# One-column modulation products placed one by one behind large products

## The chip, the cores and the metric

The kernel runs on one core of a Trainium2 chip. The metric is the device time of one execution in microseconds (us); the value compared is the median of several executions. TensorE (PE) multiplies, VectorE (DVE), ScalarE (ACT) and GpSimd (POOL) do the elementwise work, and SyncE (SP) issues most DMAs. PEld is the part of TensorE that loads weights while a product streams.

## The reference

One encoder layer on 512 tokens of width 2048 in fp32. What the change touches is the beginning: the modulation and the modulated LayerNorm, whose result h feeds every input projection.

```python
mod = jax.nn.silu(c) @ w_ada[l] + b_ada[l]
shift, scale, gate = jnp.split(mod[:, None, :], 3, axis=-1)
h = _layernorm(x) * (1.0 + scale) + shift
proj = h @ w_in[l]
# ... gated MLP on one half of proj, windowed attention on the other
y = jnp.concatenate([y_a, y_b], axis=-1) @ w_out[l]
x = _layernorm(DEEPNORM_ALPHA * x + (1.0 + gate) * y, ln_g[l], ln_b[l])
```

## The kernel before

The contraction dimension of 2048 is cut into 16 slices of 128 channels. h is kept transposed, one tile of 128 channels x 512 tokens for each slice, as two fp32r numbers `h_hi` + `h_lo`; each weight tile is split likewise into `whi` + `wlo` (or `xhi`, `xlo`): the DMA fills `raw`, ACT copies it to `whi` (L199), DVE or POOL subtracts (L201). Every product of the projections is then three "large" TensorE products of 512 (L229) or 256 columns (L242).

In the first part of the program, up to some 217 us, h is not there yet. The projections start with slices 0 and 1 and proceed in segments (`segment`), a segment for each pair of slices; while a segment runs, the modulation of the next pair is prepared. For a pair k0, k0+1 this is:

- `ada_vector`: 16 DVE multiply-adds (L384, L386) over `wada` tiles, and a last addition (L392) that leaves partial sums over 128 partitions in `scratch[1]`, a part of `gate1`.
- `ada_end`: four products of the partial sums with a column of ones (L400) add up the partitions. They are plain fp32, 128 weights columns and one streamed column each, and give shift and scale of the two slices as four columns of a PSUM tile `pc`. DVE adds the bias into `modc` (L401).
- `make_h`: ACT applies shift and scale (L416) and copies to `h_hi` (L417), DVE makes `h_lo` (L418).

There are seven such groups of four, for k0 = 2, 4, ... 14. The text calls them groups 1 to 7.

`pc` comes from `bank()`, which hands out the ring `psx`. Up to 217 us this ring has two PSUM banks (`ps_x`, bufs=2). The same ring serves the partial sums of the projections (`sums`): each sum of six or twelve large products fills one bank, and is then added into SBUF by DVE (L497) or copied by ACT (L491, L494), which frees the bank. The vz products (L242 and some of L229) instead go to four `psm` banks that they keep.

The order on each engine is made when the program is built: a scheduler places instructions by their dependencies and its own estimate of times, and picks the bank of a tile that is free first by that estimate. Instructions marked `pin` keep their order in the program. The first part of the program hands control from `segment` to `prepare` by a count of steps (L545 to L552), one `advance(1)` for each `yield`. Engines work through their instructions in order, so an instruction that waits holds up all that stand behind it on its engine.

Of the kernel before, what the change touches and what calls it, by code (L numbers as in the profile page):

```python
# [2 lines left out]

# [9 lines left out]
ALU = mybir.AluOpType  # L13
# [3 lines left out]
P = 128  # L17
# [54 lines left out]
def hybrid_kernel(ctx: ExitStack, tc: tile.TileContext, x, c, w_ada, b_ada_cols, b_gate, w_in,  # L72
                  sgu_g, sgu_b, w_sp, b_sp, rpb, band_mask, w_out, ln_g, ln_b, out):
    nc = tc.nc
    pin = tc.keep_in_program_order
# [10 lines left out]
    def bank(ring="x"):  # L86
        turn[0] += ring == "m"
        pool = rings[ring][turn[0] % 5 == 0 if len(rings[ring]) > 1 else 0]
        return pool.tile([P, T], F32, name="ps" + ring, tag=ring)
# [9 lines left out]
    bada = const.tile([P, 2, NK], F32, name="bada")  # L99
# [4 lines left out]
    one = ones.bitcast(F32)[:, 0:1]  # L104
# [15 lines left out]
    def tok(t):  # L120
        return slice(t * P, (t + 1) * P)
# [82 lines left out]
    def next_ws(n):  # L204

        while at[1] < len(plan) and len(ready) < depth[0] + (at[1] < BEFORE_LAST):
            split_w()
        return [ready.pop(0) for _ in range(n)]

    def next_w():  # L210
        return next_ws(1)[0]

    def mm3(ps, wl, i, kl, chan_major, first, last, part=slice(0, T), of=lambda i: slice(i, T, 4)):

        hi, lo, k0, widths = wl
        kk = k0 + kl
        col, o = i * P if chan_major else part.start, 0
        for w in widths:
            if col < w:
                break  # L220
            col, o = col - w, o + 2 * w
        cs = slice(o + kl * w + col, o + kl * w + (col + P if chan_major else part.stop))
        if chan_major:
            trip = ((hi[:, cs], h_hi[:, kk, :]), (hi[:, cs], h_lo[:, kk, :]), (lo[:, cs], h_hi[:, kk, :]))
        else:
            t_hi, t_lo = h_hi[:, kk, of(i)], h_lo[:, kk, of(i)]
            trip = ((t_hi, hi[:, cs]), (t_hi, lo[:, cs]), (t_lo, hi[:, cs]))
        for j, (a, b) in enumerate(trip):
            nc.tensor.matmul(ps, lhsT=a, rhs=b, start=first and j == 0, stop=last and j == 2)  # L229

    def mm_vz(ps, wl, i, kl, first, last):

        if i >= 2:
            mm3(ps, wl, i, kl, True, first, last)
            return
        hi, lo, k0, (w, _) = wl
        cs = slice(kl * w, (kl + 1) * w)

        for t in range(2):
            a_hi, a_lo = [h[:, k0 + kl, tok(2 * i + t)] for h in (h_hi, h_lo)]  # L240
            for j, (a, b) in enumerate(((a_hi, hi), (a_hi, lo), (a_lo, hi))):
                nc.tensor.matmul(ps[:, t * w:(t + 1) * w], lhsT=a, rhs=b[:, cs], start=first and t == 0 and j == 0,  # L242
                                 stop=last and t == 1 and j == 2)

    def project(kind, evac):

        pss = [bank("m") for _ in range(4)]
        for ch in range(8):
            wl = next_w()
            for i in range(4):  # L250
                for kl in range(2):
                    ends = ch + kl == 0, ch == 7 and kl == 1
                    if kind == "vz":
                        mm_vz(pss[i], wl, i, kl, *ends)
                    else:
                        mm3(pss[i], wl, i, kl, kind == "c", *ends)
                if ch == 7:
                    evac(i, pss[i])
                yield
# [28 lines left out]
    def vz_products(wl, last, evac=None):  # L288

        for i in range(4):  # L290
            for kl in range(2):
                mm_vz(res[i], wl, i, kl, False, last and kl == 1)
            if last:
                evac(i, res[i])
            yield
# [18 lines left out]
    scratch = [gate1[:, i * T:(i + 1) * T] for i in range(4)]  # L314

    with tc.tile_pool(name="ph1", bufs=1) as ph1:
# [25 lines left out]
        modc = ph1.tile([P, 2, NK], F32, name="modc")  # L342
# [51 lines left out]
        def ada_end(k0, nk):  # L394

            pc = acc_ps[0][:, T - 2:] if nk == 1 else bank()[:, :4]
            pc = pc.rearrange("p (s k) -> p s k", s=2)
            for s in range(2):
                for i in range(nk):
                    nc.tensor.matmul(pc[:, s, i:i + 1], lhsT=scratch[1][:, (nk * s + i) * P:(nk * s + i + 1) * P], rhs=one, start=True, stop=True)  # L400
            nc.vector.tensor_tensor(out=modc[:, :, k0:k0 + nk], in0=pc, in1=bada[:, :, k0:k0 + nk], op=ALU.add)  # L401
            yield
            for kk in range(k0, k0 + nk):
                make_h(kk, nk == 1)
                yield

        def make_h(kk, direct=False):

            xn = xt[:, :, kk * P:(kk + 1) * P]
            h_hi_k, h_lo_k = [h[:, kk, :].rearrange("p (n k) -> p n k", n=NT) for h in (h_hi, h_lo)]  # L410
            sc, bi = modc[:, 1, kk:kk + 1], modc[:, 0, kk:kk + 1]
            if direct:
                nc.scalar.activation(out=h_hi_k, in_=xn, func=AF.Identity, scale=sc, bias=bi)  # L413
                pin(nc.vector.tensor_scalar(out=xn, in0=xn, scalar1=sc, scalar2=bi, op0=ALU.mult, op1=ALU.add))
            else:
                nc.scalar.activation(out=xn, in_=xn, func=AF.Identity, scale=sc, bias=bi)  # L416
                nc.scalar.copy(out=h_hi_k, in_=xn)  # L417
            nc.vector.tensor_tensor(out=h_lo_k, in0=xn, in1=h_hi_k.bitcast(F32), op=ALU.subtract)  # L418

        def prepare():  # L420
            yield from ada_both(0)
            make_h(0, True)
            yield
            yield from ada_vector(1, 1)
            yield from ada_end(1, 1)
            before = iter(())
            for k0 in EVEN[1:]:
                yield from ada_vector(k0, 2, before)
                yield
                before = ada_end(k0, 2)  # L430
            yield from before
# [67 lines left out]
        def sums(q, wls, i, seg):  # L499

            ps = bank()
            for n, wl in enumerate(wls):
                for kl in range(2):
                    mm3(ps, wl, i, kl, accs[q][1], n + kl == 0, n == len(wls) - 1 and kl == 1)
                if n < len(wls) - 1:
                    yield
            sum_evac(q, i, ps, seg)
            yield

        def first_segment():  # L510

            wz, wv = next_ws(2)
            for i in range(4):
                mm_vz(res[i], wz, i, 0, True, False)
            two = [bank() for _ in range(2)]
            for i in range(2):
                mm3(two[i], wv, i, 0, False, True, False)
            advance(6)
            for i in range(4):
                mm_vz(res[i], wz, i, 1, False, False)  # L520
            yield
            for i in range(2):
                mm3(two[i], wv, i, 1, False, False, True)
                sum_evac(V, i, two[i], 0)
                yield
            for i in range(2, 4):
                yield from sums(V, [wv], i, 0)
            for q in SEGMENTS[0][1][2:]:
                wls = next_ws(1)
                for i in range(4):  # L530
                    yield from sums(q, wls, i, 0)
# [339 lines left out]
    with tc.tile_pool(name="ph3", bufs=1) as ph3:  # L871
# [46 lines left out]
        for cg in range(4):  # L918
            last = cg == 3
# [102 lines left out]
```

## Time and profile before

| what | value |
|---|---|
| median of 3 runs (909.05 to 910.12) | 909.17 us |
| the profiled execution: time | 911.18 us |
| the profiled execution: span from first to last instruction | 909.3 us |
| PE busy | 872.9 us, 96% of the span |
| DVE / ACT / POOL busy | 596.1 / 321.3 / 313.7 us |
| granted TensorE clock, mean | 0.987 of full |

The clock is at full (2.4 GHz) from 50 us on, up to the last stretch. From the page one reads which engine is busy throughout, from the chain of waits which engine's work the end follows from, and from the timeline of a few microseconds what each product costs and what it waits for. A product's record is longer than the step to the next one, because records overlap: steps are read as the difference of two starts.

### The profile page before, as it was taken

Reading aid. Unit: us, or ns where it says so; the run is one execution under the profiler, and the core shown is the slowest. Engines: PE = TensorE matmul, PEld = TensorE weight load, DVE = VectorE, ACT = ScalarE, POOL = GpSimd, SP = SyncE. Lnnn points to the kernel's source line nnn. Section 1 sums busy time; section 2 is a strip of 40 time slices with the busy share of each in tenths; the row PEclk is TensorE's granted clock in tenths of the full one; section 3 lists DMA queues with packets and bytes.
Section 4 is the critical chain, followed back from the end, with each engine's and each line's share of the span. In section 5 each row is a group of like instructions: output and inputs, shape, how many; then the busy total and the mean of one; then the engine's idle time right before and its main releaser. Section 6 shows DMA issues by size and latency. Waiting matters only on the chain.

```text
span 909.3 us, 11756 instructions
## 1 busy us (share of the span) xinstructions
PE 872.9 (96%) x4444; PEld 758.2 (83%) x4444; DVE 596.1 (66%) x864; ACT 321.3 (35%) x397; POOL 313.7 (35%) x223
## 2 busy tenths in 40 slices
PE   4799999999999999999999999999999999999993
PEld 3688888887988988898889988998888888888883
DVE  7867899634586546767768677867866625252667
ACT  3363333233641434515262515433262521122200
POOL 5436566236431526044344525252420000000035
PEclk9799999999999999999999999999999999999997
DMA  9999889744332233444454354444342282323213
GB/s 296 334 356 315 280 275 289 220 115 141 99 97 85 79 99 101 137 135 155 128 182 153 113 182 149 144 120 128 112 126 98 87 353 97 108 97 116 70 61 125
DMA packets 107499, 144.56 MB, mean 159 GB/s; under 512 B 7217, under 2 KB 79025, under 8 KB 106673
## 3 DMA queue, kind: packets, MB, share of 16 engines
q1 hardware_dynamic: 103120, 134.25, 46.4%
q10 hardware_dynamic: 4322, 9.55, 3.1%
q8 instruction: 35, 0.57, 0.3%
q14 instruction: 22, 0.18, 0.1%
HBM read 139.58 MB, written 4.19 MB: 158 GB/s over the span
## 4 chain that ended last, share of the span: by engine, by line
PE 64%; POOL 2%; issue 1%; DVE 1%; ACT 1%; DMA 0%; POOLq 0%; SPq 0%; DVEq 0%; ACTq 0%
PE psm L229 52%; PE psm L242 7%; POOL xr L901 1%; PE psx L712 1%; PE psx L664 1%; PE psx L591 1%; PE psx L663 1%; PE psx L710 1%; POOL xr L902 1%; PE psx L711 1%; POOL rs L126 0%; DMA raw<-in_w_in_dram 0%; ACT xr L900 0%; DVE wlo L201 0%; POOLq L1017 0%
## 5 line engine op out<-in xcount | busy, mean ns | idle before, releaser
L199 ACT CAST whi<-raw 128x1024 fp32r<-128x1024 f32 x133 | 139.3, 1050 | 349.6 <-PE psm L229 223.0
L201 DVE TENSOR_TENSOR wlo<-raw,whi 128x1024 fp32r<-128x1024 f32 x94 | 130.2, 1388 | 162.2 <-ACT whi L199 154.3
L229 PE MATMUL psm<-h_hi,whi 128*128 128x512 f32 x444 | 175.5, 396 | 0.4 <-DVE klo L617 0.4
L229 PE MATMUL psm<-h_lo,whi 128*128 128x512 f32 x444 | 173.9, 392 | 0.0
L229 PE MATMUL psm<-h_hi,wlo 128*128 128x512 f32 x444 | 173.8, 391 | 0.0
L201 POOL TENSOR_TENSOR wlo<-raw,whi 128x1024 fp32r<-128x1024 f32 x39 | 93.9, 2412 | 100.4 <-ACT whi L199 76.3
L229 PE MATMUL psm<-whi,h_hi 128*128 128x512 f32 (+1 forms) x296 | 114.7, 388 | 0.0
L229 PE MATMUL psm<-wlo,h_hi 128*128 128x512 f32 (+1 forms) x296 | 114.0, 385 | 0.0
L229 PE MATMUL psm<-whi,h_lo 128*128 128x512 f32 (+1 forms) x296 | 114.0, 385 | 0.0
L229 PEld LDWEIGHTS psm<-h_hi,wlo 128*128 128x128 f32 x444 | 83.8, 189 | 18.0
L229 PEld LDWEIGHTS psm<-h_hi,whi 128*128 128x128 f32 x444 | 83.9, 189 | 16.2 <-issue 0.8
L229 PEld LDWEIGHTS psm<-h_lo,whi 128*128 128x128 f32 x444 | 84.1, 189 | 15.3 <-issue 0.2
L242 PE MATMUL psm<-whi,h_hi 128*128 128x256 f32 x248 | 71.7, 290 | 2.8 <-ACT h_hi L413 2.3
L126 POOL TENSOR_TENSOR rs<-vareps,mhalf 128x1 f32<-128x1 f32 x4 | 4.1, 1026 | 203.5 <-DVE vareps L125 203.5
L386 DVE SCALAR_TENSOR_TENSOR ada<-wada,c_sb,ada 128x512 f32<-128x512 f32 (+1 forms) x104 | 68.9, 713 | 6.8 <-DMA wada<-in_w_ada_dram 6.8
L242 PE MATMUL psm<-whi,h_lo 128*128 128x256 f32 x248 | 70.9, 288 | 1.0 <-DVE h_lo L418 1.0
L242 PE MATMUL psm<-wlo,h_hi 128*128 128x256 f32 x248 | 71.1, 287 | 0.2 <-POOL wlo L201 0.2
L229 PEld LDWEIGHTS psm<-wlo,h_hi 128*128 128x128 f32 x296 | 63.5, 215 | 8.5
L229 PEld LDWEIGHTS psm<-whi,h_lo 128*128 128x128 f32 x296 | 63.4, 214 | 8.5
L229 PEld LDWEIGHTS psm<-whi,h_hi 128*128 128x128 f32 x296 | 63.4, 214 | 8.4
L229 PE MATMUL psx<-h_hi,whi 128*128 128x512 f32 x160 | 63.6, 397 | 1.2 <-DVE y_b L497 0.9
L229 PE MATMUL psx<-h_lo,whi 128*128 128x512 f32 x160 | 62.4, 390 | 0.0
(206 smaller groups left out, 1612.2 us busy)
## 6 DMA issues: line engine op xcount, KB each, us to landing
wada<-in_w_ada_dram SPq DMA_DIRECT2D x128, 256.0 KB, 5.9
raw<-in_w_in_dram SPq DMA_DIRECT2D x128, 256.0 KB, 3.1
raw<-in_w_in_dram SPq DMA_DIRECT2D x48, 512.0 KB, 4.1
rawg<-in_w_ada_dram SPq DMA_DIRECT2D x32, 512.0 KB, 4.3
raw<-in_w_out_dram SPq DMA_DIRECT2D x32, 512.0 KB, 3.6
xt<-in_x_dram SPq DMA_DIRECT2D x8, 512.0 KB, 7.7
xr<-in_x_dram ACTq DMA_DIRECT2D x4, 1024.0 KB, 8.9
tt<-in_rpb_dram ACTq DMA_DIRECT2D x16, 128.0 KB, 2.1
```

Source lines behind the costliest of these rows:

```text
L199: nc.scalar.copy(out=hi, in_=raw)
L201: eng.tensor_tensor(out=low, in0=raw, in1=hi.bitcast(F32), op=ALU.subtract)
L229: nc.tensor.matmul(ps, lhsT=a, rhs=b, start=first and j == 0, stop=last and j == 2)
L242: nc.tensor.matmul(ps[:, t * w:(t + 1) * w], lhsT=a, rhs=b[:, cs], start=first and t == 0 and j == 0, stop=last and t == 1 and j == 2)
L386: nc.vector.scalar_tensor_tensor(out=even if j == NK - 2 else acc, in0=wt[:, j - j0], scalar=cj, in1=acc, op0=ALU.mult, op1=ALU.add)
L591: nc.tensor.matmul(ps[:, tok(n)], lhsT=v[n][:, tok(g)], rhs=wsT[:, g, :], start=True, stop=True)
L663: nc.tensor.matmul(po, lhsT=k2[:, h, keys], rhs=q2[:, h, q], start=True, stop=False)
L664: nc.tensor.matmul(po, lhsT=klo[:, h, keys], rhs=q2[:, h, q], start=False, stop=True)
L710: nc.tensor.matmul(ps[:, q], lhsT=v_hi[:, t, h, :], rhs=hi[:, sl], start=t == 0, stop=False, skip_group_check=True)
L711: nc.tensor.matmul(ps[0:64, q], lhsT=v_lo[:, t, h, :], rhs=hi[:, sl], start=False, stop=False, skip_group_check=True)
L712: nc.tensor.matmul(ps[:, q], lhsT=v_hi[:, t, h, :], rhs=lo[:, sl], start=False, stop=t == 3, skip_group_check=True)
L901: nc.gpsimd.tensor_tensor(out=xr[:, t, cs], in0=xr[:, t, cs], in1=gl[:, cs], op=ALU.mult)
```

## The change

Of the four products and the addition of each group, `ada_end` no longer issues five instructions in a row. It puts them into a list `beside`. Every large product (in `mm3` and `mm_vz`) now goes through `next_beside`: if the list holds something, the large product is pinned and the first entry is issued behind it. So one product stands behind each of the next four large products, and the addition is issued behind the fifth. What is still listed when `prepare` is resumed is issued at once. The pair that is handled as single slices (nk == 1, before the groups) keeps its order, now pinned.

```diff
+    beside = []
+
+    def next_beside(large):
+        if beside:
+            pin(large)
+            beside.pop(0)()
...
-            nc.tensor.matmul(ps, lhsT=a, rhs=b, start=first and j == 0, stop=last and j == 2)
+            next_beside(nc.tensor.matmul(ps, lhsT=a, rhs=b, start=first and j == 0, stop=last and j == 2))
...
-            for s in range(2):
-                for i in range(nk):
-                    nc.tensor.matmul(pc[:, s, i:i + 1], lhsT=scratch[1][:, (nk * s + i) * P:(nk * s + i + 1) * P], rhs=one, start=True, stop=True)
-            nc.vector.tensor_tensor(out=modc[:, :, k0:k0 + nk], in0=pc, in1=bada[:, :, k0:k0 + nk], op=ALU.add)
-            yield
+
+            def product(s, i):
+                pin(nc.tensor.matmul(pc[:, s, i:i + 1], lhsT=scratch[1][:, (nk * s + i) * P:(nk * s + i + 1) * P], rhs=one, start=True, stop=True))
+
+            def columns():
+                nc.vector.tensor_tensor(out=modc[:, :, k0:k0 + nk], in0=pc, in1=bada[:, :, k0:k0 + nk], op=ALU.add)
+            todo = [partial(product, s, i) for s in range(2) for i in range(nk)] + [columns]
+            if nk == 1:
+                for f in todo:
+                    f()
+            else:
+                beside.extend(todo)
+            yield
+            while beside:
+                beside.pop(0)()
```

What the scheduler makes of it is shown at two places. Lines of the changed kernel differ: its L238 is L229 of before, L409 is L400, L200 is L199, L435 is L416, L436 is L417, L510 is L491. A name's last number tells one tile from another, and each `psx` number is one use of a bank.

TensorE at group 3, before: psx_1040 is the sum that ends, psx_1048 holds the four products, psx_1054 is the next sum.

```order
L229 MATMUL psx_1040<-h_hi_90,wlo_877 128x512
L400 MATMUL psx_1048<-ones_75,gate1_92 128x1 [waits DVE_49]
L400 MATMUL psx_1048<-ones_75,gate1_92 128x1 x3
L229 MATMUL psx_1054<-h_hi_90,whi_876 128x512 [waits DVE_49]
L229 MATMUL psx_1054<-h_lo_91,whi_876 128x512
```

The same place in the changed kernel, where psx_1049 is the next sum:

```order
L238 MATMUL psx_1040<-h_hi_90,wlo_877 128x512
L238 MATMUL psx_1049<-h_hi_90,whi_876 128x512 [waits DVE_49]
L409 MATMUL psx_1048<-ones_75,gate1_92 128x1 [waits DVE_49]
L238 MATMUL psx_1049<-h_lo_91,whi_876 128x512
L409 MATMUL psx_1048<-ones_75,gate1_92 128x1
L238 MATMUL psx_1049<-h_hi_90,wlo_877 128x512
```

The next sum now begins ahead of the first product, and two uses of the ring are open side by side while the sum before is still to be emptied. In the built programs psx_1048 had the bank other than that of psx_1040 before, and has the bank of psx_1040 now.

ScalarE behind group 1, before (y_b is the destination of the sums, xt and h_hi belong to slices 2 and 3, xhi to a later weight tile):

```order
L491 COPY s<-psx 128x512 x2
L416 ACTIVATE xt<-xt,modc 128x4x128 x2
L491 COPY y_b_108<-psx 128x512
L417 CAST h_hi<-xt 128x512 x2
L491 COPY y_b_108<-psx 128x512
L199 CAST xhi<-raw 128x1024
```

The same place in the changed kernel:

```order
L510 COPY s<-psx 128x512 x2
L510 COPY y_b_108<-psx 128x512
L435 ACTIVATE xt<-xt,modc 128x4x128 x2
L200 CAST xhi<-raw 128x1024
L436 CAST h_hi<-xt 128x512
L510 COPY y_b_108<-psx 128x512
L436 CAST h_hi<-xt 128x512
```

Shift and scale now come behind one more copy, and the copy to h_hi behind the cast of xhi. On TensorE the first product that reads h of slice 2 (L242, the vz products) stands behind 18 large products counted from the group, where it stood behind 24.

## Rows read from the trace of the kernel before

**Rows 1.** The page: busy time of an engine, and the chain that ended last.

```profile
PE 872.9 (96%) x4444; PEld 758.2 (83%) x4444; DVE 596.1 (66%) x864; ACT 321.3 (35%) x397; POOL 313.7 (35%) x223
PE 64%; POOL 2%; issue 1%; DVE 1%; ACT 1%; DMA 0%; POOLq 0%; SPq 0%; DVEq 0%; ACTq 0%
```

**Rows 2.** The line of the products: durations in ns, first and last start.

```profile
L400 PEld LDWEIGHTS psx<-ones,gate x56: 186/192/192, 61.0 to 201.6; 128*128 128x128 f32 x56
```

**Rows 3.** Timeline at group 6: start, duration (us), engine, line, operation.

```profile
182.12 0.39 PE L229 MATMUL psx<-h_hi,wlo 128*128 128x512 f32 x1
182.12 1.08 PEld L400 LDWEIGHTS psx<-ones,gate 128*128 128x128 f32 x8
182.34 0.95 PE L400 MATMUL psx<-ones,gate 128*128 128x1 f32 x8
183.12 0.19 PEld L229 LDWEIGHTS psx<-h_hi,whi 128*128 128x128 f32 x1
183.24 0.19 PEld L229 LDWEIGHTS psx<-h_lo,whi 128*128 128x128 f32 x1
...
184.16 0.39 PE L229 MATMUL psx<-h_lo,whi 128*128 128x512 f32 x1
```

**Rows 4.** Timeline at group 3.

```profile
109.87 0.39 PE L229 MATMUL psx<-h_hi,wlo 128*128 128x512 f32 x1
110.29 0.69 DVE L497 TENSOR_TENSOR y_a<-psx,y_a 128x512 f32<-128x512 f32 x1
111.04 0.50 PE L229 MATMUL psx<-h_hi,whi 128*128 128x512 f32 x1
...
112.08 0.39 PE L229 MATMUL psx<-h_lo,whi 128*128 128x512 f32 x1
```

**Rows 5.** Timeline at group 4.

```profile
133.62 0.69 DVE L497 TENSOR_TENSOR s<-psx,s 128x512 f32<-128x512 f32 x1 [0.59 <-PE psx L229]
134.37 0.31 PEld L229 LDWEIGHTS psx<-whi,h_hi 128*128 128x128 f32 x1
...
135.54 0.40 PE L229 MATMUL psx<-wlo,h_hi 128*128 128x512 f32 x1
```

**Rows 6.** Timelines at groups 1, 2 and 7: the emptying, then the fifth large product.

```profile
61.41 0.59 ACT L491 COPY s<-psx 128x512 f32<-128x512 f32 x1 [0.70 <-PE psx L229]
63.45 0.40 PE L229 MATMUL psx<-h_lo,whi 128*128 128x512 f32 x1
...
86.26 0.59 ACT L494 COPY gate<-psx 128x512 f32<-128x512 f32 x1 [0.49 <-PE psx L229]
88.12 0.39 PE L229 MATMUL psx<-h_lo,whi 128*128 128x512 f32 x1
...
201.23 0.69 DVE L497 TENSOR_TENSOR s<-psx,s 128x512 f32<-128x512 f32 x1 [2.03 <-PE psx L229]
203.01 0.39 PE L229 MATMUL psx<-h_lo,whi 128*128 128x512 f32 x1
```

**Rows 7.** Timeline of PE at 215 us, where the ring is closed.

```profile
215.52 0.39 PE L229 MATMUL psx<-h_hi,wlo 128*128 128x512 f32 x1
216.78 0.47 PE L229 MATMUL psx<-h_hi,whi 128*128 128x512 f32 x1 [0.88 <-DVE y_b L497]
```

**Rows 8.** Timelines of ACT and PE behind group 1.

```profile
62.39 1.52 ACT L416 ACTIVATE xt<-xt,modc 128x512 f32<-128x512 f32 x2 [0.40 <-DVE modc L401]
64.59 1.14 ACT L417 CAST h_hi<-xt 128x512 fp32r<-128x512 f32 x2
66.11 1.06 ACT L199 CAST xhi<-raw 128x1024 fp32r<-128x1024 f32 x1
67.99 0.28 PE L242 MATMUL psm<-whi,h_hi 128*128 128x256 f32 x1
```

**Rows 9.** Timeline at 173 us: DVE waits for a DMA, PE for DVE.

```profile
173.03 1.42 DVE L386 SCALAR_TENSOR_TENSOR ada<-wada,c_sb,ada 128x512 f32<-128x512 f32 x2 [2.76 <-DMA wada<-in_w_ada_dram]
...
175.09 0.63 PE L229 MATMUL psx<-whi,h_hi 128*128 128x512 f32 x1 [1.65 <-DVE s L497]
```

More of the change, by code (lines that the diff above doesn't have):

```diff
@@ L1 @@
 from contextlib import ExitStack
+from functools import partial
 from itertools import chain
@@ L241, in mm_vz @@
             for j, (a, b) in enumerate(((a_hi, hi), (a_hi, lo), (a_lo, hi))):
-                nc.tensor.matmul(ps[:, t * w:(t + 1) * w], lhsT=a, rhs=b[:, cs], start=first and t == 0 and j == 0,
-                                 stop=last and t == 1 and j == 2)
+                next_beside(nc.tensor.matmul(ps[:, t * w:(t + 1) * w], lhsT=a, rhs=b[:, cs], start=first and t == 0 and j == 0,
+                                             stop=last and t == 1 and j == 2))
     def project(kind, evac):
```

## The prediction

> **What bounds the kernel now.** I read the page first: PE is busy for 96% of the span, and its own work is 64% of the chain that ended last, with no other engine above 2% [rows 1]. So the end moves when PE's stream gets longer or shorter, and I price the change there alone. Next came the line of the products: 56 loads for 28 products, two loads to each [rows 2]. Then I went group by group through the timelines of PE, and asked of each what PE does between the large product that ends one sum and the fifth large product behind it; the changed order has by then issued the same instructions. DVE and ACT came last, since they empty the ring's banks and make h.
>
> **What a product costs.** Group 6 is undisturbed [rows 3]. The next sum's first large product begins when the load for the second starts, at 183.24, and the fifth is at 184.16: a step from one large product to the next is 0.92 / 4 = 0.23 us. In the group each load is 0.19 us long, but loads follow each other faster: from 182.34, where the large product's successor begins, to 183.12 are seven loads, (183.12 − 182.34) / 7 = 0.111 us, and 183.24 − 183.12 is the same. The products' one streamed column vanishes beside that. The first load of the group starts with the last large product at 182.12 and hides under it; the other seven, and the load of the next large product, are exposed. So a group costs 8 × 0.11 = 0.89 us.
>
> **The same products one by one.** Behind a large product, the first load of a single product hides. Its second load, and the load of the large product behind it, have only a one-column product to hide under, and are exposed: 2 × 0.11 = 0.22 us, and four times that is 0.89 us again. The mere taking apart brings nothing. In group 6 I get 184.13 for the fifth large product where it stood at 184.16 [rows 3]; in group 5 likewise −0.02. (A step from large to large with a product between is 0.23 + 0.22 = 0.45 us.) What decides is where the products now find their bank.
>
> **The ring of two banks.** Before, the four products took the bank that had been empty for some time, and while they ran, the sum that had just ended was emptied: group 3 has the last large product at 109.87, the emptying from 110.29 to 110.98, and the next sum's first large product at 111.04, 0.06 us behind it [rows 4]. The products are the cover of that emptying. In the changed order the next sum starts first, in the bank that is free, and the products need the bank of the sum that has just ended. So PE issues one large product and then waits for the emptying, with everything behind the first product in line. The wait ends at the same moment as before; call it W, the end of the emptying plus 0.06. But now the four products are still to come. From W: three exposed loads, 0.33 us, until the second large product starts, then three steps of 0.45, so the fifth large product is at W + 1.67. By group:
>
> - Group 1: ACT ends at 61.41 + 0.59 = 62.00, W = 62.06, fifth large 63.73 against 63.45 [rows 6], +0.28. (Before, PE waited here for the addition of the bias too, so less is lost.)
> - Group 2: 86.26 + 0.59, W = 86.91, 88.58 against 88.12 [rows 6], +0.46.
> - Group 3: W = 111.04, 112.71 against 112.08 [rows 4], +0.63.
> - Group 4: 133.62 + 0.69, W = 134.37. Here h is the weights operand with a stride of four tokens and its load is 0.31 long, not 0.19 [rows 5]. From W to the fifth large product are 1.17 us here and 1.04 in group 3 [rows 4], so an exposed one of these costs 0.13 more. One of them is in each step: the second large product is at W + 0.45, three steps of 0.57 follow, in all 136.53 against 135.54 [rows 5], +0.99.
> - Groups 5 and 6: the large products go to psm banks, or the sum keeps its bank: −0.02 and −0.03.
> - Group 7: 201.23 + 0.69, W = 201.97, 203.64 against 203.01 [rows 6], +0.63.
>
> The sum is +2.9 us. The trace of before shows one wait of just this kind, where the ring is closed at 215 us: PE stands 0.88 us for the emptying by DVE [rows 7]. Five such waits would be 4.4 us, an upper bound for this term; the lower one is nothing, if the emptying begins so early that a large product covers it (it takes 0.59 to 0.69, a large product 0.23).
>
> **h comes later behind group 1.** The addition stands behind the fifth large product now, at about 63.9 to 64.06; before, shift and scale began at 62.39, after 0.40 of waiting for it [rows 8]. ACT then does in order: one copy of a sum (0.59 by [rows 6], until 64.94, since PE ends that sum at about 64.3), shift and scale (1.52), the cast of xhi (1.06), and the first copy to h_hi (1.14 / 2 = 0.57), which makes 68.09. Before, that copy was ready at 64.59 + 0.57 = 65.2 and first read at 67.99 [rows 8], 2.8 us of slack. PE now comes to it after 18 large products from the group instead of 24: 63.73 + 14 × 0.23 = 66.95. It waits 68.09 − 66.95 = 1.14 us, about +1.15. Bounds: nothing, if ACT takes the copies earlier by 1.1 us; 2.1, if the cast of xhi itself is late by another microsecond. I take the sum of the rows. In the other groups h is ready before PE reads it, as I follow it there.
>
> **DVE at 173 us.** An emptying stands there behind multiply-adds that wait 2.76 us for a DMA, and PE waits 1.65 for it [rows 9]. In the changed order one more multiply-add stands ahead of that emptying, but one wada DMA is issued earlier. I take 0, with bounds of −1.65 (the wait goes) and +1.2 (one multiply-add of 0.71 and its DMA's delay).
>
> **The sum.** 2.9 + 1.15 = 4.1 us. The profiled execution was 911.18, so its counterpart would be 915.3; it lay 2.0 above the median of 909.17 (its span leaves 1.9 outside). On the median: 909.17 + 4.1 = **913.3 us**. The bounds of the first two terms give 910.4 to 915.8.
>
> Of what a load may hide under, the trace shows that each starts when the matmul before it starts, one ahead [rows 3]. The Trainium skill, "TensorE: Matmul & The Clock Gate", section "Step-by-step: what each phase is for", says that PE's queue pulls a weight load ahead of running matmuls into a background buffer, so that the next weights load while this product runs. If that reached two loads ahead, a large product would cover both loads of a product; eight loads in a row in group 6, at even distances, speak against it.
>
> **Rivals.**
>
> 1. *A large product covers two loads.* Place: all 28 products; price: one load of 0.111 less for each, −3.1 us. The sum is then +1.0, 910.2 us: not slower by anything that can be told. What can be told is about 0.2%, 1.8 us. It decides once 21 of the 28 products save a load (4.1 − 21 × 0.111 = 1.8). For it: a large product lasts 0.23 and two loads take 0.22. Against it: the even spacing in [rows 3]. A chance of 0.15.
> 2. *h is in time at group 1.* ACT's casts are placed such that shift, scale and the first h_hi come through by 66.9. Then only the ring's part is left: 909.17 + 3.0 = 912.1. For it: 2.8 us of slack before. Against it: the cast of xhi, which is now ahead in ACT's order. A chance of 0.18.
> 3. *DVE's queue at 173 us gets later*, by the extra multiply-add: +1.2, 914.5. For it: PE already waits there [rows 9], so all of it is paid. Against: the DMA that ends the wait is issued earlier. A chance of 0.12.
> 4. *The wait at 173 us goes*, since the DMA that ends it starts earlier, and the change does not do what it says at the ring: there the emptying has run under the large product that now stands first. Then −1.65 + 1.15 or less, 908.7 and below. Against it: an emptying of 0.6 to 0.7 doesn't fit under 0.23. A chance of 0.05.
>
> The forecast keeps 0.50, with a range of its own of 912.3 to 914.1. Cases 2 and 3 are slower too: 0.80 in all. Within 0.2%: 0.15. Faster: 0.05, for rival 4. The range of 8 in 10 takes in the upper half of what rival 1 may give, and leaves out the rest of it, rival 4, and the far ends of the bounds: 910.6 to 914.8.
>
> **What the changed profile must show.** At groups 1 to 4 and 7, the first product waits for DVE or ACT (0.3 to 0.7 us idle of PE, the releaser the emptying), at 5 and 6 not. Steps of 0.45 us between large products with a product between, 0.57 at group 4; steps near 0.34 would mean rival 1. A wait of PE of about 1 us for ACT's h_hi near 67 us; without it, rival 2. Near 173 us a wait between 0 and 2.9. If products stand with no wait at the ring, the bank is not the one I read in the built programs, and the sum loses 2.9.

## The result and the profile after

The changed kernel takes 917.27 us (median of 6 executions, 915.14 to 920.40) where the kernel before took 909.28 beside it: a ratio of 1.009 with a 95% interval of 1.0072 to 1.0107. Three further measurements gave ratios of 1.0078, 1.0089 and 1.009. I had forecast 913.3 and a range up to 914.8: the direction was right, the size half of what came, and the range too narrow.

The page of the changed kernel hardly shows it (parts 1 and 4). PE is busy for the same share of the span as before [rows 1], and has the same share of the chain that ended last:

```profile
PE 876.4 (96%) x4444; PEld 758.9 (83%) x4444; DVE 600.7 (66%) x864; ACT 321.2 (35%) x397; POOL 313.7 (34%) x223
PE 64%; POOL 2%; issue 1%; DVE 1%; ACT 1%; DMA 0%; POOLq 0%; SPq 0%; DVEq 0%; ACTq 0%
```

The list of PE's waits up to 225 us (who waited for whom: us in total, times, longest) shows what is new. Before, this list held the 1.65 us wait of [rows 9], the 0.88 us wait of [rows 7], and 0.3 us for the addition. The products themselves (L409) now wait, in five places, each time for the emptying of a sum, and PE waits for h_hi, h_lo and a second time for a sum y_b:

```profile
PE psx L238 <- DVE s L516: 1.7, 1, 1.7
PE psx L238 <- DVE y_b L516: 1.6, 2, 0.9
PE psx L409 <- DVE s L516: 1.2, 2, 0.6
PE psm L251 <- ACT h_hi L436: 0.8, 1, 0.8
PE psx L409 <- DVE y_a L516: 0.6, 1, 0.6
PE psx L409 <- ACT s L510: 0.5, 1, 0.5
PE psx L409 <- ACT gate L513: 0.4, 1, 0.4
PE psm L251 <- DVE h_lo L437: 0.2, 1, 0.2
```

Group 3 on PE's timeline (start, duration, engine, line, operation), to be held against [rows 4]: one large product, the wait, and then single products with large ones between them.

```profile
111.44 0.39 PE L238 MATMUL psx<-h_hi,whi 128*128 128x512 f32 x1
112.38 0.38 PE L409 MATMUL psx<-ones,gate 128*128 128x1 f32 x2 [0.56 <-DVE y_a L516]
112.63 0.49 PE L238 MATMUL psx<-h_lo,whi 128*128 128x512 f32 x1
...
113.09 0.47 PE L238 MATMUL psx<-h_hi,wlo 128*128 128x512 f32 x1
...
114.00 0.47 PE L238 MATMUL psx<-h_lo,whi 128*128 128x512 f32 x1
```

From the end of the wait, at 112.38, to the fifth large product at 114.00 are 1.62 us; I had reckoned 1.67 from W. The step between large products with a product between them is 113.09 − 112.63 = 0.46, forecast 0.45.

**The ledger.** PE issues the large products in nearly the same order in both kernels. So one can number them, leave the one-column products out, and take the difference of start times of the same number in the two traces: where that difference rises, time is lost. Below, each column is one traced execution of the changed kernel against the first trace of before (a step is the rise between two such numbers, in us). Products of 256 columns start 0.12 us apart and those of 512 columns 0.23, and the two orders mix them differently behind groups 1 and 2; there a row ends where both kernels have issued the same products. Group 4 is counted to its fifth large product, the other groups to the sixth, which comes a step of 0.32 instead of 0.23 behind the fifth.

| place | forecast | trace 1 | trace 2 | trace 3 | trace 4 |
|---|---|---|---|---|---|
| start of the program, to 61 us | 0 | −1.62 | −1.67 | −0.48 | +3.58 |
| group 1 | +0.28 | 0.30 | 0.30 | 0.31 | 0.30 |
| h behind group 1, to 73 us | +1.15 | 1.53 | 1.52 | 1.53 | 1.52 |
| 73 to 86 us | 0 | 0.27 | 0.28 | 0.27 | 0.25 |
| group 2 | +0.46 | 0.47 | 0.48 | 0.48 | 0.46 |
| 89 to 99 us | 0 | 0.39 | 0.38 | 0.39 | 0.40 |
| group 3 | +0.63 | 0.67 | 0.66 | 0.67 | 0.66 |
| group 4 | +0.99 | 0.82 | 0.81 | 0.81 | 0.81 |
| behind group 4, the next ten large products, the sixth first | 0 | **1.74** | 0.22 | 0.22 | 0.22 |
| the wait at 173 us | 0 | 0.03 | −1.22 | 0.14 | 0.74 |
| group 7 | +0.63 | 0.67 | 0.67 | 0.67 | 0.67 |
| behind group 7 | 0 | 0.69 | −0.07 | 0.18 | 0.32 |
| groups 5, 6 and all else | −0.05 | 0.07 | 0.10 | 0.12 | 0.19 |
| sum behind 61 us | +4.1 | 7.65 | 4.13 | 5.79 | 6.54 |
| time of this execution | | 917.20 | 913.64 | 916.46 | 921.26 |

### The profile page after: what moved, and what is told of

It reads as the page before. It is cut to its first block, busy times and chain, and to the rows that moved or that the text cites. A ratio compares the mean times of both kernels' runs of the same rounds, so it can differ in the third digit from the quotient of the medians.

```text
span 915.4 us, 11754 instructions
## 1 busy us (share of the span) xinstructions
PE 876.4 (96%) x4444; PEld 758.9 (83%) x4444; DVE 600.7 (66%) x864; ACT 321.2 (35%) x397; POOL 313.7 (34%) x223
## 4 chain that ended last, share of the span: by engine, by line
PE 64%; POOL 2%; issue 1%; DVE 1%; ACT 1%; DMA 0%; POOLq 0%; SPq 0%; DVEq 0%; ACTq 0%
PE psm L238 52%; PE psm L251 7%; POOL xr L920 1%; PE psx L731 1%; PE psx L683 1%; PE psx L610 1%; PE psx L682 1%; PE psx L729 1%; POOL xr L921 1%; PE psx L730 1%; POOL rs L127 0%; DMA raw<-in_w_in_dram 0%; ACT xr L919 0%; DVE wlo L202 0%; POOLq L1036 0%
## 5 line engine op out<-in xcount | busy, mean ns | idle before, releaser
L200 ACT CAST whi<-raw 128x1024 fp32r<-128x1024 f32 x133 | 139.2, 1050 | 347.0 <-PE psm L238 229.9
L238 PE MATMUL psm<-h_hi,whi 128*128 128x512 f32 x444 | 175.6, 396 | 0.4 <-DVE klo L636 0.4
L238 PE MATMUL psm<-h_hi,wlo 128*128 128x512 f32 x444 | 173.8, 392 | 0.0
L238 PE MATMUL psm<-h_lo,whi 128*128 128x512 f32 x444 | 173.7, 391 | 0.0
L238 PE MATMUL psm<-whi,h_hi 128*128 128x512 f32 (+1 forms) x296 | 114.7, 388 | 0.0
L238 PE MATMUL psm<-wlo,h_hi 128*128 128x512 f32 (+1 forms) x296 | 114.0, 385 | 0.0
L238 PE MATMUL psm<-whi,h_lo 128*128 128x512 f32 (+1 forms) x296 | 114.0, 385 | 0.0
L238 PEld LDWEIGHTS psm<-h_hi,wlo 128*128 128x128 f32 x444 | 83.6, 188 | 17.8
L238 PEld LDWEIGHTS psm<-h_hi,whi 128*128 128x128 f32 x444 | 84.0, 190 | 16.0 <-issue 0.8
L238 PEld LDWEIGHTS psm<-h_lo,whi 128*128 128x128 f32 x444 | 83.9, 189 | 15.4 <-issue 0.2
L251 PE MATMUL psm<-whi,h_hi 128*128 128x256 f32 x248 | 71.8, 291 | 3.6 <-ACT h_hi L432 2.3
L251 PE MATMUL psm<-whi,h_lo 128*128 128x256 f32 x248 | 70.6, 288 | 1.1 <-DVE h_lo L437 1.1
L251 PE MATMUL psm<-wlo,h_hi 128*128 128x256 f32 x248 | 70.9, 287 | 0.0
L238 PEld LDWEIGHTS psm<-wlo,h_hi 128*128 128x128 f32 x296 | 63.5, 215 | 8.5
L238 PEld LDWEIGHTS psm<-whi,h_lo 128*128 128x128 f32 x296 | 63.4, 214 | 8.5
L238 PEld LDWEIGHTS psm<-whi,h_hi 128*128 128x128 f32 x296 | 63.4, 214 | 8.4
L238 PE MATMUL psx<-h_hi,whi 128*128 128x512 f32 x160 | 63.2, 395 | 1.6 <-DVE y_b L516 1.6
L238 PE MATMUL psx<-h_hi,wlo 128*128 128x512 f32 x160 | 62.9, 393 | 0.4 <-POOL wlo L202 0.4
```

The lines of the kernel that those rows point to most:

```text
L200: nc.scalar.copy(out=hi, in_=raw)
L238: next_beside(nc.tensor.matmul(ps, lhsT=a, rhs=b, start=first and j == 0, stop=last and j == 2))
L251: next_beside(nc.tensor.matmul(ps[:, t * w:(t + 1) * w], lhsT=a, rhs=b[:, cs], start=first and t == 0 and j == 0, stop=last and t == 1 and ...
```

## Experiments

All are short edits of the changed kernel. The times beside them are medians; before took 909.3 to 910.1 in the same sittings. Lines of code that aren't shown are those of the diff ahead.

**The changed kernel three more times** (no edit).

> The changed kernel once more, for a second trace and a tighter time. Theory A (the fall of the granted clock to half at 139.0 to 142.4 us, behind group 4, belongs to the changed order there): the clock falls at the same place again, and the time is about 8 us above before. Rival B (the fall is an event of one execution): no fall at group 4, or one somewhere else, and a time that scatters by some 1.7 us (3.4 us at half speed) from run to run.

> The changed kernel a third time, to see one of its longer executions (918 to 920 us) in a trace. Theory A: the longer ones have a fall of the clock at group 1 too (62 to 70 us), where PE stands still for the ring and then for h, and lose 1.7 us or twice that by it. Rival B: they have the clock of the others there, and lose the time in waits for DMAs or DVE further on (at 173 us up to 1.7, at 228 us 0.7).

> The changed kernel, a fourth trace. Theory A: without a fall of the clock 4 to 6 us of PE's steps behind 60 us more than before, with one at group 4 1.7 us on top; the waits at the groups, behind group 1 and at 95 us as in its other traces. Rival B: the waits themselves differ between executions by a microsecond or more, so that the sum read from one trace says little.

They took 917.13, 918.14 and 918.68 us (ratios of 1.0078, 1.0089 and 1.009) and gave traces 2 to 4 of the table. The losses at the groups, behind group 1 and at 95 us agree to 0.03 us in all four: they belong to the order. Four things differ between executions: the start of the program, the wait at 173 us, what follows group 7 (in trace 1 PE waits there for POOL's `wlo`), and what follows group 4. Trace 1 against trace 2 is the reading for that last one. PE's timeline of trace 1, at group 4 and behind it:

```profile
136.51 0.38 PE L409 MATMUL psx<-ones,gate 128*128 128x1 f32 x2 [0.55 <-DVE s L516]
136.75 0.60 PE L238 MATMUL psx<-wlo,h_hi 128*128 128x512 f32 x1
...
137.33 0.60 PE L238 MATMUL psx<-whi,h_lo 128*128 128x512 f32 x1
...
139.31 0.63 PE L238 MATMUL psx<-whi,h_hi 128*128 128x512 f32 x1
139.74 0.63 PE L238 MATMUL psx<-wlo,h_hi 128*128 128x512 f32 x1
...
142.58 0.40 PE L238 MATMUL psx<-whi,h_lo 128*128 128x512 f32 x1
142.81 0.40 PE L238 MATMUL psx<-whi,h_hi 128*128 128x512 f32 x1
```

Within the group the step is 137.33 − 136.75 = 0.58, as forecast (0.57). Behind it, it is 0.43 at 139.3 and 0.23 at 142.6, and nothing is waited for. The busy times by stretch (start:end, length, then PE, PEld, DVE, ACT, POOL, the granted clock, DMA share, GB/s) say why: the clock fell to half, 1.2 GHz, between 139 and 142, behind a stretch in which PE worked 3.45 of 4 us and had the slow steps of group 4.

```profile
135.00:139.00 4.00, 3.45 (x18) 3.01 (x17) 1.69 (x4) 0.32 (x2) 2.36 (x1) 1.00 0.28 89
139.00:142.00 3.00, 3.00 (x9) 2.35 (x9) 1.77 (x3) 2.41 (x4) 0.00 (x0) 0.50 0.95 298
```

That is 1.74 − 0.22 = 1.5 us of the 7.65. In traces 2 to 4 the same waits are there and the clock holds, so theory A (the fall belongs to the order and comes each time) is wrong as I put it: the fall came in one of these four. What the third trace was to catch, a longer execution with a fall at group 1, wasn't caught. The longest, trace 4, lost its time elsewhere: at the start of the program, 3.58 us. There the clock of 40 to 50 us was lower than in trace 3 (the columns as above; trace 4 first, then trace 3):

```profile
40.00:50.00 10.00, 7.76 (x26) 6.39 (x27) 8.90 (x14) 1.75 (x2) 2.36 (x1) 0.51 1.10 349
```

```profile
40.00:50.00 10.00, 10.00 (x37) 9.00 (x38) 8.93 (x15) 3.75 (x5) 3.93 (x2) 0.73 1.10 350
```

**All groups but the fourth, and the fourth alone.** One condition in `ada_end` each: the group is issued at once.

```diff
-            if nk == 1:
+            if nk == 1 or k0 == 8:      (all but group 4)
+            if k0 != 8:                 (group 4 alone)
```

> The changed order everywhere but at group 4, whose four products stand together again. Theory A (clock fall is caused at group 4): the fall goes, and with it 1.74 us, and the wait and the exposed strided loads of group 4, 0.82: 2.6 us below the changed kernel, some 5.4 us above before. Rival B (the fall is not tied to group 4): 0.8 us below the changed kernel, and the clock falls in another place.

> The kernel before with the changed order at group 4 alone. Theory A: +0.85 us for the wait on the emptied bank and the order of the loads, and +1.74 us for a fall of the clock behind it: +2.6 us. Rival B (no fall without the other groups): +0.85 us, and a clock that stays at full from 50 us on.

> The kernel with the changed order at group 4 alone, a second trace. Theory A: the clock falls at group 4 again in this kernel (its seven times lay within 1.5 us, at 2.2 us above before, which only holds with a fall in nearly all), +2.2 us. Rival B: no fall in this trace, and the 2.2 us are found in steps or waits elsewhere.

Without group 4: 915.28 (ratio 1.0059, 1.0047 to 1.0071), no fall of the clock behind 50 us up to the last stretch, 1.9 us below the changed kernel's 917.13, between theory A's 2.6 and rival B's 0.8. Group 4 alone: 912.08 (1.0026, 1.0016 to 1.0037), and the clock fell at 135.3 us; in the second trace, of a measurement at 911.41 (1.0012, 1.0000 to 1.0024), it held. The two traces in the stretch of the fall, first and second:

```profile
135.00:139.00 4.00, 4.00 (x13) 3.28 (x12) 1.62 (x4) 2.55 (x4) 0.00 (x0) 0.57 0.85 260
```

```profile
135.00:139.00 4.00, 4.00 (x20) 3.91 (x19) 1.97 (x4) 2.38 (x4) 0.42 (x1) 1.00 0.56 168
```

In the ledger the group itself costs 0.82 and 0.81 in both. The fall needs no other group, and comes in some executions. With the changed order at group 4 it was in two of seven traces (the four above, these two, and that of all groups but the first, below). In the ten traces with group 4 as before, or with its products together, there was none, three traces of before among them. Two of seven against none of ten does not settle whether the order at group 4 makes a fall likelier. And a fall does not need that order: both kernels with a slow DVE, below, had one at 133 us, ahead of group 4, and one of them has all its groups together.

**The first group alone, and all but the first.** The same condition, with k0 == 2.

> The kernel before with the changed order at group 1 alone. Theory A (the ring costs 0.30 there, and h_hi and h_lo of slices 2 and 3 come too late behind ScalarE's cast of xhi, 1.6): +1.9 us, with a wait of PE of some 0.8 us for ScalarE's copy to h_hi. Rival B (h is late only because of something further on or of this execution): +0.3 us, and no such wait.

> The kernel with group 1 alone in the changed order once more, for the same question: two of its eight executions were 3 us above the others. Theory A: in such an execution the clock falls between 62 and 75 us. Rival B: the clock stays at full, and a wait elsewhere is longer. If the profile falls on one of the common executions: no fall, and +2.6 us against before in PE's own steps, as in its first trace.

> The changed order everywhere but at group 1, whose four products stand together again. Theory A (group 1 alone costs 2.6 us: the ring 0.3, h_hi and h_lo late 1.6, a later sum of y_b at 95 us 0.6; and the runs some 3 us above the others, seen in the changed kernel and in the one with group 1 alone, come from group 1 too): some 4.7 us below the changed kernel's median, +3 to +4 us against before, no run that stands 3 us above the others. Rival B (the scattered runs come from elsewhere): about 2.6 us below the changed kernel, with runs 3 us apart still there.

Group 1 alone: 912.68 (1.0035, 1.0022 to 1.0048) and 912.42 (1.0023, 1.0011 to 1.0034). The ledger has 0.31 and 0.30 for the ring, 1.52 for h, 0.28 up to 86 us, and then 0.30 between 89 and 99. All but group 1: 913.21 (1.0034, 1.0022 to 1.0047), with 0.14 us between 89 and 99. In the ledger the two parts add up to the whole to 0.05 us there, and most of the loss at 95 us comes with group 1, though it lies 30 us behind it; but PE waits 0.51 us for that emptying without group 1 too. The medians don't add up: the parts are 2.3 to 3.0 and 3.1 us above before, the whole 7.4 to 8.8. None of these three traces shows a clock below full at group 1, so the executions 3 us above the others (before has such ones too, 913.1 to 913.5 in three of 23) stay without an explanation from this place; trace 4 suggests the start of the program, and does not prove it.

**Together, but at the new place.** All four products behind the first large product of the next sum; empty entries keep the next large products in their order.

```diff
-                beside.extend(todo)
+                beside.extend([lambda: [f() for f in todo]] + 4 * [lambda: None])
```

> All four products of each group together, right behind the first large product of the next sum (that large product and the four behind it are kept in this order). Theory A (the place is what costs, by the wait for the bank; being apart costs nothing): PE waits at groups 1 to 4 and 7 as in the changed kernel, the groups cost 2.9 to 3.0 us together, the addition comes three large products earlier and h behind group 1 costs less than 1.6: between +3 and +5 us against before, with falls of the clock behind group 4 in some executions. Rival B (being apart costs by itself): the same waits, but 1 us or more cheaper in the groups than the changed kernel, and no fall of the clock.

> The kernel before with group 4 alone placed so: its four products together, right behind the first large product of the next sum. Theory A (the clock falls because of the stretch without streamed columns, and that is as long whether the products are apart or together): +0.85 us in the group and +1.7 us for a fall of the clock in most executions, about what group 4 alone cost in the changed order, 2.4 us. Rival B (a stretch of slow steps with single products is what takes the clock down): +0.85 us and no fall.

All groups: 913.90 (1.0047, 1.0029 to 1.0066). Group 4 alone (k0 != 8 at once): 910.91 (1.0013, 1.0002 to 1.0023). PE at group 3, which is at the same place as in the changed kernel to 0.03 us:

```profile
111.47 0.39 PE L238 MATMUL psx<-h_hi,whi 128*128 128x512 f32 x1
112.42 1.05 PE L409 MATMUL psx<-ones,gate 128*128 128x1 f32 x8 [0.56 <-DVE y_a L516]
113.33 0.48 PE L238 MATMUL psx<-h_lo,whi 128*128 128x512 f32 x1
...
114.11 0.40 PE L238 MATMUL psx<-h_lo,whi 128*128 128x512 f32 x1
```

The wait is the same, 0.56, and the fifth large product is at 114.11 here and at 114.00 there. In the ledger the groups cost 0.29, 0.46, 0.65, 0.66 and 0.69, where the products apart cost 0.30, 0.47, 0.67, 0.82 + 0.22 and 0.67. So standing apart is free, as worked out, except at group 4 with its strided loads: 0.38 us more. What the changed kernel loses beyond this one lies behind the groups: h behind group 1 costs 0.87 here and 1.53 there, the 0.27 up to 86 us isn't there, and between 89 and 99 us this kernel gains 0.18 where that one loses 0.39. PE does not wait for h_hi here; it waits 0.59 us for h_lo. The clock held in both traces; with one execution each that tells little on whether a fall is likelier with products apart.

**A bank of their own.** The odd multiply-adds accumulate in SBUF, and the bank that this sets free takes the four columns. Once with the products apart, once together at the old place.

```diff
-            accs = [t[:, :2 * w].rearrange("p (s w) -> p s w", s=2) for t in acc_ps]
+            ...
+            if nk == 2:
+                accs[1], even = even, accs[0]
-            pc = acc_ps[0][:, T - 2:] if nk == 1 else bank()[:, :4]
+            pc = acc_ps[0][:, T - 2:] if nk == 1 else acc_ps[1][:, :4]
```

> The changed order, but the four columns get a PSUM bank of their own (the odd multiply-adds accumulate in SBUF, which sets that bank free). Theory A (the ring of two banks is what the products wait for): no wait at any group, eight exposed loads in each, the five groups cost 0.1 to 0.3 us less than before each instead of 2.95 more together, and no fall of the clock behind group 4, since PE does not stand still there. The late h behind group 1 stays (up to 1.6): between -1 and +1.5 us against before. Rival B (single products cost by themselves, by their loads or by the clock): +3 us or more, and steps of more than 0.45 us.

> The order before (four products together), with the same bank of their own. Theory A: a control for the accumulation in SBUF, and what is left of waits on the ring in the groups of before (0.12 to 0.34 us at five groups) goes: -1.2 to 0 us. Rival B (the multiply-adds get longer with one accumulator in SBUF and DVE's queue is later for the sums): +0.5 us or more, with longer waits of PE for DVE.

They took 923.85 and 925.37 us, far above theory A of either: the price of the accumulation in SBUF, which rival B of the second names, drowned the rest. The groups of multiply-adds on DVE (line, operation, count, busy, mean ns, idle before), with the accumulator in SBUF and in PSUM:

```profile
L397 DVE SCALAR_TENSOR_TENSOR gate<-wada,c_sb,gate 128x512 f32<-128x512 f32 x49 | 64.3, 1312 | 0.0
L397 DVE SCALAR_TENSOR_TENSOR ada<-wada,c_sb,ada 128x512 f32<-128x512 f32 (+1 forms) x62 | 41.8, 689 | 0.0
```

The means, 1.31 and 0.69, mix cases (and 0.69 two shapes). With the accumulator in SBUF, the 22 of the 49 that had POOL idle beside them took 0.74 us, and the 25 beside which POOL worked for at least half of their time took 1.85 on average and up to 2.87. With it in PSUM, all 49 of 128 x 512 took 0.74 to 0.76, POOL at work or not. So DVE fell behind, PE waited for its sums, and in these two the clock fell at 133 us. But at the groups the readings are clean. Group 3 with the products apart, where no product waits:

```profile
116.72 0.39 PE L238 MATMUL psx<-h_hi,whi 128*128 128x512 f32 x1
116.94 0.28 PE L411 MATMUL ada<-ones,gate 128*128 128x1 f32 x2
117.08 0.48 PE L238 MATMUL psx<-h_lo,whi 128*128 128x512 f32 x1
```

In the ledger groups 1, 2, 3, 4 and 7 cost −0.42, −0.25, −0.17, −0.01 and −0.22: 1.1 us less than before, where the ring made them 2.9 us more. That is the direct evidence for the ring. Behind group 1, 1.60 us still go for h, but in another way: PE waits 1.3 us for h_lo and not for h_hi.

**Together and late.** If the four products hang on the first large product without anything kept behind it, the scheduler sets them behind two to six large products of the next sum.

```diff
-                beside.extend(todo)
+                beside.append(lambda: [f() for f in todo])
```

> All four products of a group stand together, but behind the first large product of the next sum, and the addition of the bias right behind them. Theory A (what costs is where they stand: the bank of the sum just ended; that they are apart costs nothing): the same waits at groups 1 to 4 and 7, fifth large product at W + 1.69 instead of W + 1.67, so +2.95 us for the groups; h of slices 2 and 3 is earlier in ScalarE's order (first copy to h_hi ahead of the cast of xhi), so the 1.6 us behind group 1 mostly go; and a clock that may fall behind group 4 as it does in the changed kernel, +1.7: between +3 and +4.7 us. Rival B (being apart is what costs): waits, but a group costs as before, +0.5 us or less.

> Four products together, and late (behind two to six large products of the next sum, which cover the emptying of its bank), except for group 1, which stands as before. Theory A (what cost in the run with all groups late was h behind group 1, 1.66 us in its trace; the late products themselves cost nothing, and the wait at 173 us for DVE goes): 1.5 to 2 us below before, and no run 3 to 4 us above the others. Rival B (the late groups bring runs with a lower clock by themselves): about as before, with some runs 3 to 4 us above the others.

All groups: 910.11 (1.0017, 1.0003 to 1.0032). All but group 1 (issued at once): 909.60 (0.9997, 0.9986 to 1.0007). I had expected waits for the ring in the first one, and there are none. Group 3, DVE and PE:

```profile
110.13 0.69 DVE L516 TENSOR_TENSOR y_a<-psx,y_a 128x512 f32<-128x512 f32 x1
...
111.06 0.39 PE L238 MATMUL psx<-h_hi,wlo 128*128 128x512 f32 x1
...
111.29 0.95 PE L409 MATMUL psx<-ones,gate 128*128 128x1 f32 x8
...
112.49 0.50 PE L238 MATMUL psx<-h_hi,whi 128*128 128x512 f32 x1 [0.26 <-DVE modc L412]
```

The emptying ends at 110.82, under the six large products that now stand ahead of the four, so the bank is free when they come. The next sum then waits for the addition, 0.26 us, as group 1 did before. Behind group 1, with all groups late, 1.69 us go for h (PE waits 1.4 for h_lo, which takes 2.46 us there); with group 1 as before, nothing. So the second version is the kernel before by its time, though its trace has no wait at 173 us. None of the versions beats the kernel before.

**The kernel before, twice more** (no edit).

> The kernel before, a second trace. Theory A (the wait at 173 us, 1.65 in its first trace, is shorter in a common execution, since the first trace is 1.5 us above the median): the wait is below 1.2 us, and PE's time behind 61 us some 1 us shorter than in the first trace. Rival B: the wait is 1.65 again, and only the start of the program was slower in the first trace.

> The same for a third trace: Theory A, a wait at 173 us below 1.2 us and no fall of the clock between 50 and 890 us; Rival B, 1.65 again.

909.94 (1.0002, 0.9992 to 1.0011) and 910.22 (1.0010, 0.9998 to 1.0023). PE's waits at 173 us in the two traces:

```profile
PE psx L229 <- DVE s L497: 1.1, 1, 1.1
```

```profile
PE psx L229 <- DVE s L497: 0.9, 1, 0.9
```

They are 0.5 and 0.6 below the 1.65 of [rows 9], and the ledger behind 61 us is −0.46 and −0.56. The trace that I had set the sum against had a long one. In the changed kernel the four traces have 1.7, 0.4, 1.8 and 2.4 here.

## Why the prediction was half right

The step that failed is the one on h: I followed it to ScalarE's h_hi and to PE's first product with it, and put at nothing what DVE needs for h_lo and what that does to the sums behind it ("In the other groups h is ready before PE reads it"). The runs show h_lo taking 2.47 us instead of 0.69 beside POOL, a second wait of PE, and 0.27 and 0.39 us lost in two places further on.

- **The cost of a product, and standing apart.** Right. Two exposed loads for each, steps of 0.46 for 0.45; the same sum together and apart, at 0.02 us for groups 1 to 3 and 7. Rival 1 would have shown steps near 0.34 with a product between; none did. The rule of the Trainium skill ("TensorE: Matmul & The Clock Gate", "Step-by-step: what each phase is for"), that loads are pulled ahead of running matmuls, agrees with these steps for one load, and not for two.
- **The ring of two banks.** Right in mechanism and places, near in size. At the fifth large product, where my sum stopped, groups 1, 2, 3, 4 and 7 cost 0.21, 0.38, 0.57, 0.81 and 0.57, where I had 0.28, 0.46, 0.63, 0.99 and 0.63. The step behind it is longer too, and with it they cost 0.30, 0.47, 0.67, 1.04 and 0.67, 3.1 us in all where I had 2.9. There is nothing at 5 and 6, and the loss is gone with a bank of their own.
- **h behind group 1.** Right in the place, too small: 1.53 for 1.15. The wait for h_hi came as worked out, but the cast of xhi that now stands ahead of it does more than take ScalarE's time. It also lets POOL begin its subtraction for xlo, and DVE makes h_lo beside that. ScalarE's, POOL's, DVE's and PE's rows of after, and DVE's and POOL's of before:

```profile
64.69 1.03 ACT L200 CAST xhi<-raw 128x1024 fp32r<-128x1024 f32 x1
65.62 0.62 ACT L436 CAST h_hi<-xt 128x512 fp32r<-128x512 f32 x1
65.80 2.40 POOL L202 TENSOR_TENSOR xlo<-raw,xhi 128x1024 fp32r<-128x1024 f32 x1 [4.73 <-ACT xhi L200]
66.27 2.47 DVE L437 TENSOR_TENSOR h_lo<-xt,h_hi 128x512 fp32r<-128x512 f32 x1 [1.88 <-ACT h_hi L436]
```

```profile
65.12 0.39 PE L238 MATMUL psx<-h_hi,wlo 128*128 128x512 f32 x1
66.29 0.39 PE L251 MATMUL psm<-whi,h_hi 128*128 128x256 f32 x1 [0.79 <-ACT h_hi L436]
...
68.26 0.39 PE L238 MATMUL psx<-h_hi,wlo 128*128 128x512 f32 x1
68.80 0.39 PE L251 MATMUL psm<-whi,h_lo 128*128 128x256 f32 x1 [0.15 <-DVE h_lo L437]
```

```profile
65.25 1.29 DVE L418 TENSOR_TENSOR h_lo<-xt,h_hi 128x512 fp32r<-128x512 f32 x2 [0.21 <-ACT h_hi L417]
67.24 2.42 POOL L201 TENSOR_TENSOR xlo<-raw,xhi 128x1024 fp32r<-128x1024 f32 x1 [4.57 <-ACT xhi L199]
```

  The step to the first L251 is 1.17 instead of 0.23, so the wait for h_hi costs 0.94, where I had 1.14. The step to the first product with h_lo is 0.54 instead of 0.12, another 0.42. With an h_lo of 0.69, as in before, h_lo would have been there at 66.96 (an estimate from these rows), long ahead of the 68.80. Before, both h_lo of this pair were made ahead of POOL's subtraction. In the 19 traces, between 60 and 230 us, the 181 h_lo that had POOL idle beside them took 0.68 to 0.70 us, and those beside which POOL worked for 0.8 us or more took 1.06 to 2.48. No run moves the cast of xhi alone, so its part is shown by these rows and not by an edit. Rival 2, h in time, was wrong.
- **What a later h does to DVE's queue.** I only asked whether h is ready before PE reads it. At 95 us the emptying of a sum y_b stands right behind an h_lo on DVE that takes 1.72 us, and PE waits 0.77 for the bank. In the trace of before that h_lo takes 1.12, the emptying runs at 93.69 behind one more multiply-add, and PE has no wait. DVE's rows and PE's, of after, and DVE's of before:

```profile
93.81 1.72 DVE L437 TENSOR_TENSOR h_lo<-xt,h_hi 128x512 fp32r<-128x512 f32 x1
95.45 1.27 DVE L516 TENSOR_TENSOR y_b<-psx,y_b 128x512 f32<-128x512 f32 x2
```

```profile
96.18 0.50 PE L238 MATMUL psx<-h_hi,whi 128*128 128x512 f32 x1 [0.77 <-DVE y_b L516]
```

```profile
91.98 1.12 DVE L418 TENSOR_TENSOR h_lo<-xt,h_hi 128x512 fp32r<-128x512 f32 x1
93.03 0.74 DVE L386 SCALAR_TENSOR_TENSOR ada<-wada,c_sb,ada 128x512 f32<-128x512 f32 x1
93.69 0.68 DVE L497 TENSOR_TENSOR y_b<-psx,y_b 128x512 f32<-128x512 f32 x1
```

  It costs 0.39 between 89 and 99 us. The length of that h_lo goes with the loss: the eight traces in which it takes 1.72 to 1.78 us lose 0.30 to 0.40 there, and those in which it takes 1.06 to 1.14 lie between −0.30 and 0.14 (the two kernels with a slow DVE left out). The 0.27 up to 86 us comes at 76.66, where PE's load waits for another emptying by DVE. I looked at DVE's order only where it waited in the trace of before, at 173 us.
- **DVE at 173 us.** I set 0, with bounds of −1.65 and +1.2. The four traces are at −1.22, 0.03, 0.14 and 0.74, and in before itself the wait scatters by 0.7. The bounds held; the reference was not typical, by 0.5.
- **The clock.** Not in the sum, and not among the rivals. "The clock is at full (2.4 GHz) from 50 us on" was read from one trace of before, and I took it as given for the changed kernel. A fall behind group 4 costs 1.5 us in the ledger (0.22 stays without it) and came in one trace of four. That the change makes it likelier is not shown.
- **The sum.** Without a fall and with the wait at 173 us left out, traces 2 to 4 give 5.35, 5.65 and 5.80 where I had 4.1; 0.4 of the difference is h behind group 1, and 0.65 the two stretches further on. Set against the mean of three traces of before (−0.34), the mean of four, 6.03, becomes 6.4 us. The measured medians are 7.4 to 8.8 us apart. The remaining 1.0 to 2.4 are **open**: the traced executions of before took 910.3 to 911.2 and stand above its medians, those of the changed kernel took 913.6 to 921.3 and lie on both sides of its own, and what the untraced ones lose was not seen. A clock that falls in more of them, and starts like that of trace 4, are the candidates; neither is shown.
- **The range.** The top, 914.8, lies just above rival 3 at 914.5. The bounds that I had written, 0 to 4.4 for the ring and 0 to 2.1 for h, add up to 909.2 to 915.7 (the prediction says 910.4 to 915.8), and I had cut them; even so they end below the 917.27.

## To carry to other kernels

A small product between two sums of a double-buffered ring is cover: as long as it takes the bank that has long been free, the emptying of the sum that just ended runs under it. Put it behind the first product of the next sum and it wants just the bank that isn't free yet; ask of each moved instruction which buffer it takes and what was hidden under it, before asking how long it lasts. And where a result comes later on one engine, follow every engine that makes something of it and what stands behind that in its queue (here h_hi, then h_lo, then the emptying of another sum), not only the next reader. Ask also what the instruction that overtook it lets another engine begin (here POOL's subtraction beside h_lo).

## What was new about the hardware

- The granted clock fell to half for 3.4 us in the middle of a program whose PE is busy for 96% of its span, behind a wait of 0.55 us and three steps of 0.58 at group 4, and from there a step of a large product took 0.43 us instead of 0.23. The same instructions with the same waits kept the full clock in other executions: three of four traces of the changed kernel, one of two with group 4 alone, the one with all groups but the first.
- Where the loads of the large products have a stride of four tokens, one-column products cost more apart: group 4 costs 0.38 us more apart than together, the other groups within 0.02 the same.
- A DVE subtraction of two SBUF tiles of 128 x 512 (h_lo) takes 0.69 us with POOL idle and took 2.47 where it began 0.47 behind a POOL subtraction of 2.40 us, ending 0.54 behind it.
- A multiply-add of 128 x 512 on DVE takes 0.74 us with its accumulator in PSUM, whatever POOL does. With the accumulator in SBUF it takes the same 0.74 while POOL is idle, and 1.85 on average, up to 2.87, beside a working POOL.
